# A decoder layer in which most PE transposes are replaced by 32x32 block transposes on VectorE and a pass through DRAM

## The chip, the cores and the metric

The kernel runs on one core of a Trainium2 chip. The metric is the device time of one execution in microseconds (us); the time before is 2097.85 us, the median of 3 runs (2097.81 to 2097.95). The engines are named as the profile names them: PE (TensorE) with PEld for its weight loads, DVE (VectorE), ACT (ScalarE), POOL (GpSimd) and SP (SyncE), which issues the DMAs.

## The reference

One decoder layer on 256 tokens, D_MODEL 2048, all in float32:

```
x = x + 1/2 * SwiGLU_1(rms(x))              # D_FF 5632: (silu(x@wg) * (x@wu)) @ wd
h = rms(x); proj = h @ w_in                 # q | k | v | u | v_sg | gate_att | gate_sg
  q, k: rotary on the first quarter of each of 12 heads (128 wide)
  branch A: causal dilated window attention, 3 groups of 4 heads, merged by denominators
  branch B: u * (W_s LN(v_sg) + b), W_s lower triangular
  merged = sigmoid(gate_att) * (A @ w_att_out) + sigmoid(gate_sg) * (B @ w_sg_out)
x = x + merged @ w_out
x = x + 1/2 * SwiGLU_2(rms(x))
out = rms(x) * final_norm
```

## The kernel before

**Products in three passes.** Each float32 matrix product is made of three float32r products: the left side is split into `hi` and `lo`, the weights into `wh` and `wl`, and PE adds hi·wh, hi·wl and lo·wh (lines 145 to 147). Activations are the stationary side, so they have to lie transposed in SBUF: 128 features on the partitions, the 256 tokens along the row. Weights are the moving side, 512 columns at a time.

**The list of half units.** All products of the layer are cut into 776 half units, numbered `i`: two 128-row slices of a weight, times two token halves, times three passes, which is 12 matmuls of 128x512. A gate, up or w_in product has 8 half units for its 512 columns, a down product 12 or 10. The main loop (lines 719 to 729) issues for each `i` the 12 matmuls, then the callbacks that were put at `i` with `at`, then the split of the weights of half unit `i + 4` (line 130 on ACT writes `wh`, line 131 on DVE writes `wl`). There are four `wh`/`wl` buffers, so the split of `i + 4` waits until PE is done with half unit `i`. A 1 MB weight load (`raw`, three buffers, line 121 on SP) is issued as soon as the split that frees its buffer stands in the list. Every engine takes its instructions in the order of this list.

**The transposes.** When a result is ready, PE transposes it in 128x128 pieces against an identity matrix into PSUM, and ACT and DVE bring it back as `hi` and `lo`. With `e` the last half unit of the product that gave the result:
- feed-forward (22 chunks of 512 columns, `post_up`): DVE multiplies at `e+1`, PE transposes 8 pieces at `e+2` (line 263), `split_psum` at `e+3` (lines 152 and 153);
- the two inner norms (`residual`, four chunks of 512 each, for n = 1 and 2): 8 transposes at `e+2` (line 179), the copies with the norm's gain at `e+3` (lines 184 and 186);
- q and k (`post_qk`, three chunks each): rotary at `e+2`, 8 transposes at `e+3` (line 434), plain copies at `e+4`;
- the merge (`post_merge`, four chunks): 8 transposes at `e+2` (line 583), `split_psum` at `e+3`.

The transposed feed-forward chunks `hhi` and `hlo` are the left side of the down products, which follow at once: half unit `e+1` of a down product reads slices 0 and 1, `e+2` slices 2 and 3, and so on. The feed-forward is done in two parts, of 6 chunks (24 slices) and of 5 chunks (20 slices). The first norm of the layer, attention and the gating branch have transposes of their own.

Of the kernel before, what the change touches and what calls it, by code (L numbers as in the profile page):

```python
# [8 lines left out]
F32 = mybir.dt.float32  # L9
F32R = mybir.dt.float32r  # L10
BF16 = mybir.dt.bfloat16
AF = mybir.ActivationFunctionType
# [29 lines left out]
def layer(ctx: ExitStack, tc: tile.TileContext, a, out):  # L42
# [2 lines left out]
    big = ctx.enter_context(tc.tile_pool(name="big", bufs=1))  # L45
    sb = ctx.enter_context(tc.tile_pool(name="sb", bufs=1))
    ps = ctx.enter_context(tc.tile_pool(name="ps", bufs=1, space=PSUM))
    ctx.enter_context(tc.manual_schedule())

    def mm_bank(name):  # L50
# [2 lines left out]
    def tp_bank(name):  # L53
        return ps.tile([P, NC], F32, tag="tp", bufs=4, name=name)
# [96 lines left out]
    def split_psum(hi, lo, src):  # L151
        ACT.activation(hi, src, AF.Copy)
        DVE.tensor_tensor(lo, src, hi.bitcast(F32), op=OP.subtract)


    xT = {}

    def norm_open(n):
# [30 lines left out]
    def residual(e, n, c, banks, scale, norm):  # L189
        cs = slice(c * NC, (c + 1) * NC)  # L190

        def add():
            for t in range(NT):
                DVE.scalar_tensor_tensor(two(x[:, t, cs]), banks[t], scale, two(x[:, t, cs]),  # L194
                                         op0=OP.mult, op1=OP.add)
            if norm:
                if c == 0:
                    norm_open(n)
                norm_squares(n, c)

        at(e + 1, add)
        if not norm:
            return
        got = {}

        def tr():
            for kk in range(2):
                ks = [4 * c + 2 * kk, 4 * c + 2 * kk + 1]
                got[kk] = ks, norm_transposes(f"{n}_{ks[0]}", ks)
            if c == 3:  # L210
                norm_rstd(n)

        def ev():
            for kk in range(2):
                norm_evac(n, *got[kk])

        at(e + 2, tr)
        at(e + 3, ev)


    def ffn(wg, wu, wd, down_post):
        halves = ((0, 6), (6, 11))
        for hf, (f0, f1) in enumerate(halves):
            st = {}

            def lhs_x():
                return xT["hi"], xT["lo"]

            def lhs_h(st=st):
                return st["hi"], st["lo"]  # L230

            for f in range(f0, f1):
                def post_gate(e, banks, st=st):
                    st["sg"] = sg = sb.tile([P, NT, NC], F32, tag="tmp", bufs=2, name=f"sg{e}")

                    def go():
                        rstd = xT["rstd"]
                        for t in range(NT):
                            ACT.activation(two(sg[:, t]), banks[t], AF.Silu, scale=rstd[:, t:t + 1])

                    at(max(e + 1, 11), go)

                def post_up(e, banks, st=st, f=f, f0=f0):
                    sg = st["sg"]
                    kl = 4 * (f - f0)
                    if f == f0:
                        st["hi"] = big.tile([P, 24, S], F32R, tag="A", name=f"hhi{e}")
                        st["lo"] = big.tile([P, 24, S], F32R, tag="B", name=f"hlo{e}")
                    got = {}

                    def mul():
                        rstd = xT["rstd"]
                        for t in range(NT):
                            DVE.scalar_tensor_tensor(two(sg[:, t]), banks[t], rstd[:, t:t + 1], two(sg[:, t]),  # L254
                                                     op0=OP.mult, op1=OP.mult)

                    def tr():
                        for kk in range(2):
                            b = tp_bank(f"ht{e}_{kk}").rearrange("p (j s) -> p j s", j=2)
                            for j in range(2):  # L260
                                for t in range(NT):
                                    k = 2 * kk + j
                                    PE.transpose(b[:, j, t * P:(t + 1) * P], sg[:, t, k * P:(k + 1) * P], ident)  # L263
                            got[kk] = b

                    def ev():
                        for kk in range(2):
                            ks = slice(kl + 2 * kk, kl + 2 * kk + 2)
                            split_psum(st["hi"][:, ks], st["lo"][:, ks], got[kk])

                    at(e + 1, mul)
                    at(e + 2, tr)
                    at(e + 3, ev)

                gemm(wg, f * NC, 0, KD, lhs_x, post_gate)
                gemm(wu, f * NC, 0, KD, lhs_x, post_up)
            for c in range(4):
                gemm(wd, c * NC, f0 * NC, 4 * (f1 - f0), lhs_h,
                     lambda e, banks, c=c, hf=hf: down_post(e, c, banks, hf == 1))
# [124 lines left out]
    def post_qk(key, gi):  # L404
        def post(e, banks):
            q = sb.tile([P, NT, NSLOT, HD], F32, tag="tmp", bufs=2, name=f"{key}{gi}")
            if ("qk", 0) not in mix:
                mix["qk", 0] = big.tile([P, 2, NG, S], F32, tag="A", name="qkT")
            dst = mix["qk", 0][:, 0 if key == "q" else 1, 4 * gi:4 * gi + 4]
            got = {}  # L410

            def cp():
                for t in range(NT):
                    ACT.activation(q[:, t].rearrange("p (a h) d -> p a (h d)", a=2), banks[t], AF.Copy,
                                   scale=xT["rstd"][:, t:t + 1])

            def rope():
                for t in range(NT):
                    tmp = sb.tile([P, NSLOT, 32], F32, tag="rope", bufs=2, name=f"rp{e}_{t}")
                    x1, x2 = q[:, t, :, 0:16], q[:, t, :, 16:32]  # L420
                    c2 = cs_t[:, t, 0:1, :].to_broadcast([P, NSLOT, 32])
                    s1 = cs_t[:, t, 1:2, 0:16].to_broadcast([P, NSLOT, 16])
                    s2 = cs_t[:, t, 1:2, 16:32].to_broadcast([P, NSLOT, 16])
                    DVE.tensor_tensor(tmp[:, :, 0:16], x2, s1, op=OP.mult)
                    DVE.tensor_tensor(tmp[:, :, 16:32], x1, s2, op=OP.mult)
                    DVE.tensor_tensor(q[:, t, :, 0:32], q[:, t, :, 0:32], c2, op=OP.mult)
                    DVE.tensor_tensor(q[:, t, :, 0:32], q[:, t, :, 0:32], tmp, op=OP.add)

            def tr():
                for hh in range(2):  # L430
                    b = tp_bank(f"{key}t{gi}_{hh}").rearrange("p (j s) -> p j s", j=2)
                    for j in range(2):
                        for t in range(NT):
                            PE.transpose(b[:, j, t * P:(t + 1) * P], q[:, t, 2 * hh + j], ident)  # L434
                    got[hh] = b

            def ev():
                ACT.activation(dst[:, 0:2], got[0], AF.Copy)
                DVE.tensor_copy(dst[:, 2:4], got[1])

            at(e + 1, cp)
            at(e + 2, rope)
            at(e + 3, tr)
            at(e + 4, ev)
            if key == "k" and gi == 2:
                attention(e + 21)
        return post
# [117 lines left out]
    def post_merge(c):  # L565
        def post(e, banks):
            post_mul("ga")(e, banks)
            ga, gs = mix["ga"], mix["gs"]
            got = {}
            if c == 0:  # L570
                mix["mhi"] = big.tile([P, KD, S], F32R, tag="A", name="mhi")
                mix["mlo"] = big.tile([P, KD, S], F32R, tag="C", name="mlo")

            def add():
                DVE.tensor_tensor(ga, ga, gs, op=OP.add)

            def tr():
                for kk in range(2):
                    b = tp_bank(f"mt{c}_{kk}").rearrange("p (j s) -> p j s", j=2)
                    for j in range(2):  # L580
                        k = 2 * kk + j
                        for t in range(NT):
                            PE.transpose(b[:, j, t * P:(t + 1) * P], ga[:, t, k * P:(k + 1) * P], ident)  # L583
                    got[kk] = b

            def ev():
                for kk in range(2):
                    ks = slice(4 * c + 2 * kk, 4 * c + 2 * kk + 2)
                    split_psum(mix["mhi"][:, ks], mix["mlo"][:, ks], got[kk])

            at(e + 1, add)
            at(e + 2, tr)
            at(e + 3, ev)
        return post
# [188 lines left out]
```

## Time and profile before

| what | value |
|---|---|
| median of 3 runs | 2097.85 us |
| profiled execution | 2098.01 us |
| its span, first to last instruction | 2096.3 us |
| granted TensorE clock, mean | 0.999 |
| PE busy | 2083.5 us (99%) |
| DVE busy | 1127.0 us (54%) |
| ACT busy | 965.2 us (46%) |
| DMA | 416.40 MB, mean 199 GB/s |

The span holds the work of all engines; the 1.7 us between it and the execution's time lie around it. The matmuls of PE are pipelined, so the durations of single matmuls overlap, and what one costs is read from the distance between starts. The granted clock is that of full speed (2.4 GHz) in nearly all of the span. Busy times of DVE and ACT can be added up.

### The profile page before, as it was taken

To read this page: it belongs to the slowest core of one execution; us is meant where nothing else is said; L and a number is where in the kernel's file an instruction comes from. 1 tells how busy PE (TensorE), PEld (TensorE's weight loads), DVE (VectorE), ACT (ScalarE), POOL (GpSimd) and SP (SyncE) were. 2 spreads that over 40 slices of the span, in tenths; PEclk is the share of its full clock that TensorE was granted. 3 is DMA by queue.
4 is the path that set the end of the run, shared out by engine and by line. 5 is a ranking of instruction groups with operands and counts; after the bars stand their busy time and mean duration, and the time that the engine had idled before them with its cause. 6 is when DMAs were issued, how large, how long until landed. Compare 5 with 4: busy or idle time off the path is not lost.

```text
span 2096.3 us, 24121 instructions
## 1 busy us (share of the span) xinstructions
PE 2083.5 (99%) x9897; PEld 1825.1 (87%) x9897; DVE 1127.0 (54%) x1141; ACT 965.2 (46%) x1090; POOL 9.4 (0%) x13
## 2 busy tenths in 40 slices
PE   9999999999999999999999999999999999999998
PEld 7888888888888888888888888888888888888887
DVE  5555555455555555655555555555555555555554
ACT  6444444444445544444454444544444444444443
POOL 0000000000000000000000000000000000000000
PEclk9999999999999999999999999999999999999999
DMA  7666655666675666556545566556665566666654
GB/s 262 200 201 201 201 200 202 201 201 201 195 251 188 201 201 201 173 189 200 190 146 186 201 201 201 201 192 198 200 199 196 200 202 204 200 200 220 201 200 141
DMA packets 210759, 416.40 MB, mean 199 GB/s; under 512 B 6685, under 2 KB 10457, under 8 KB 210521
## 3 DMA queue, kind: packets, MB, share of 16 engines
q1 hardware_dynamic: 210648, 414.87, 59.8%
q8 instruction: 77, 1.26, 0.2%
q14 instruction: 34, 0.27, 0.0%
HBM read 412.74 MB, written 2.10 MB: 198 GB/s over the span
## 4 chain that ended last, share of the span: by engine, by line
PE 99%; DMA 0%; issue 0%; ACT 0%; DVE 0%; SPq 0%; ACTq 0%; POOLq 0%; POOL 0%
PE mm L146 32%; PE mm L145 32%; PE mm L147 32%; PE ht L263 1%; PE xt L179 0%; DMA raw<-in_ffn_w_gate_dram 0%; PE sc L473 0%; PE sp L376 0%; PE mt L583 0%; PE pv L521 0%; PE pv L520 0%; PE pv L516 0%; PE sc L471 0%; PE kt L434 0%; PE pt L500 0%
## 5 line engine op out<-in xcount | busy, mean ns | idle before, releaser
L131 DVE TENSOR_TENSOR wl<-raw,wh 128x1024 fp32r<-128x1024 f32 (+1 forms) x777 | 949.8, 1223 | 937.7 <-ACT wh L130 935.8
L130 ACT ACTIVATE wh<-raw 128x1024 fp32r<-128x1024 f32 (+1 forms) x777 | 818.7, 1055 | 1070.9 <-PE mm L147 1055.7
L145 PE MATMUL mm<-wh,xhi 128*128 128x512 f32 x2144 | 818.2, 382 | 0.6 <-ACT wh L130 0.6
L146 PE MATMUL mm<-wl,xhi 128*128 128x512 f32 x2144 | 813.0, 379 | 0.5 <-DVE wl L131 0.5
L147 PE MATMUL mm<-wh,xlo 128*128 128x512 f32 x2144 | 812.6, 379 | 0.0
L146 PEld LDWEIGHTS mm<-wl,xhi 128*128 128x128 f32 x2144 | 405.3, 189 | 57.8 <-DVE wl L131 1.4
L147 PEld LDWEIGHTS mm<-wh,xlo 128*128 128x128 f32 x2144 | 405.2, 189 | 57.4
L145 PEld LDWEIGHTS mm<-wh,xhi 128*128 128x128 f32 x2144 | 405.3, 189 | 57.2 <-ACT wh L130 1.0
L145 PE MATMUL mm<-wh,hhi 128*128 128x512 f32 x704 | 267.6, 380 | 0.0
L146 PE MATMUL mm<-wl,hhi 128*128 128x512 f32 x704 | 266.8, 379 | 0.0
L147 PE MATMUL mm<-wh,hlo 128*128 128x512 f32 x704 | 266.8, 379 | 0.0
L147 PEld LDWEIGHTS mm<-wh,hlo 128*128 128x128 f32 x704 | 133.1, 189 | 18.9
L145 PEld LDWEIGHTS mm<-wh,hhi 128*128 128x128 f32 x704 | 133.1, 189 | 18.7
L146 PEld LDWEIGHTS mm<-wl,hhi 128*128 128x128 f32 x704 | 133.1, 189 | 18.6
L145 PE MATMUL mm<-wh,mhi 128*128 128x512 f32 x128 | 48.8, 382 | 0.0
L146 PE MATMUL mm<-wl,mhi 128*128 128x512 f32 x128 | 48.5, 379 | 0.0
L147 PE MATMUL mm<-wh,mlo 128*128 128x512 f32 x128 | 48.5, 379 | 0.0
L145 PE MATMUL mm<-wh,uT 128*128 128x512 f32 x96 | 36.7, 383 | 0.0
L146 PE MATMUL mm<-wl,uT 128*128 128x512 f32 x96 | 36.4, 379 | 0.0
L147 PE MATMUL mm<-wh,uT 128*128 128x512 f32 x96 | 36.4, 379 | 0.0
L254 DVE SCALAR_TENSOR_TENSOR sg<-mm,rstd,sg 128x512 f32<-128x512 f32 x44 | 30.9, 743 | 0.0
L165 ACT ACTIVATE junk<-x 128x512 bf16<-128x512 f32 x30 | 18.9, 629 | 21.3 <-DVE x L194 15.1
(140 smaller groups left out, 668.0 us busy)
## 6 DMA issues: line engine op xcount, KB each, us to landing
raw<-in_w_in_dram SPq DMA_DIRECT2D x92, 1024.0 KB, 4.9
raw<-in_ffn_w_up_dram SPq DMA_DIRECT2D x88, 1024.0 KB, 5.0
raw<-in_ffn_w_down_dram SPq DMA_DIRECT2D x88, 1024.0 KB, 5.0
raw<-in_ffn_w_gate_dram SPq DMA_DIRECT2D x85, 1024.0 KB, 5.1
raw<-in_w_out_dram SPq DMA_DIRECT2D x16, 1024.0 KB, 5.0
raw<-in_w_sg_out_dram SPq DMA_DIRECT2D x12, 1024.0 KB, 5.0
raw<-in_w_att_out_dram SPq DMA_DIRECT2D x4, 1024.0 KB, 5.0
raw<-in_ffn_w_gate_dram SPq DMA_DIRECT2D x5, 512.0 KB, 7.9
```

The source lines that it names most:

```text
L130: ACT.activation(wh[:, k], r[:, k], AF.Copy)
L131: DVE.tensor_tensor(wl[:, k], r[:, k], wh[:, k].bitcast(F32), op=OP.subtract)
L145: PE.matmul(o, hi[:, k, tt], in_turn(wh[:, jj]), start=first, stop=False)
L146: PE.matmul(o, hi[:, k, tt], in_turn(wl[:, jj]), start=False, stop=False)
L147: PE.matmul(o, lo[:, k, tt], in_turn(wh[:, jj]), start=False, stop=last)
L165: ACT.activation(junk, x[:, t, c * NC:(c + 1) * NC], AF.Square, accum_out=ss[n][:, t, c:c + 1])
L254: DVE.scalar_tensor_tensor(two(sg[:, t]), banks[t], rstd[:, t:t + 1], two(sg[:, t]), op0=OP.mult, op1=OP.mult)
L263: PE.transpose(b[:, j, t * P:(t + 1) * P], sg[:, t, k * P:(k + 1) * P], ident)
```

## The change

A helper `turn` takes the place of the transposes in `post_up`, in `post_qk`, and in chunks 0 to 2 of the inner norms and of the merge: 22 + 6 + 6 + 3 = 37 places. Chunk 3 of the norms and of the merge stays on PE, as do the first norm, attention and the gating branch. A turn does this:
- at its first point, two DVE instructions transpose the 32x32 blocks of a 128x1024 result (one per token half) into a tile `d` in SBUF, and SP writes `d` to a DRAM tile in one DMA of 512 KB;
- three half units later, SP reads it back in four DMAs of 128 KB, each to 32 partitions, in runs of 1 KB;
- six half units after the first point, ACT and DVE write `hi` and `lo` (or, for q and k, plain copies) from the SBUF tile that was read back. For the norms four ACT instructions multiply by the gain before that.

```
+    def turn(i, name, src, dst, ev):
+        got = {}
+        def blocks():
+            d = sb.tile([P, 4, 4, NT, 32], F32, tag="gate", bufs=2, name=f"bt{name}")
+            v = src()
+            for t in range(NT):
+                DVE.transpose(d.rearrange("p j k t b -> p t k j b")[:, t],
+                              v[:, t].rearrange("p (k j b) -> p k j b", j=4, b=32))
+            m = got["m"] = dram.tile([P, 4, S], F32, tag="turn", name=f"bm{name}")
+            SP.dma_start(m, d.rearrange("p j k t b -> p j (k t b)"))
+        def back():
+            got["e"] = e = dst()
+            m = got["m"].rearrange("(i a) j r -> j a i r", a=32)
+            for j in range(4):
+                SP.dma_start(e[32 * j:32 * j + 32].rearrange("p t c -> p (t c)").rearrange("p (i r) -> p i r", i=4),
+                             m[j])
+        at(i, blocks)
+        at(i + 3, back)
+        at(i + 6, lambda: ev(got["e"].rearrange("p t c -> p (t c)").rearrange("p (i q b) -> p q i b", i=4, b=32)))
+    def turned(ap):
+        return ap.rearrange("p k (t i b) -> p (k t) i b", t=NT, b=32)
...
@@ residual @@
+        if c < 3:
+            def evac(src):
+                for j in range(4):
+                    v = src[:, 2 * j:2 * j + 2]
+                    k = 16 * n + 4 * c + j
+                    ACT.activation(v, v, AF.Copy, scale=gcols[:, k:k + 1])
+                ks = slice(4 * c, 4 * c + 4)
+                split_psum(turned(xT["hi"][:, ks]), turned(xT["lo"][:, ks]), src)
+            turn(e + 2, f"x{n}_{c}", lambda: x[:, :, cs],
+                 lambda: sb.tile([P, NT, NC], F32, tag="gate", bufs=2, name=f"xt{n}_{c}"), evac)
+            return
...
@@ post_up @@
-                    at(e + 2, tr)
-                    at(e + 3, ev)
+                    turn(e + 2, f"h{e}", lambda: sg, lambda: sg, ev)
...
@@ post_qk @@
-                ACT.activation(dst[:, 0:2], got[0], AF.Copy)
-                DVE.tensor_copy(dst[:, 2:4], got[1])
+            def ev(src):
+                ACT.activation(turned(dst[:, 0:2]), src[:, 0:4], AF.Copy)
+                DVE.tensor_copy(turned(dst[:, 2:4]), src[:, 4:8])
...
-            at(e + 3, tr)
-            at(e + 4, ev)
+            turn(e + 3, f"{key}{gi}", lambda: flat(q), lambda: flat(q), ev)
...
@@ post_merge @@
+            if c < 3:
+                turn(e + 2, f"m{c}", lambda: ga, lambda: ga,
+                     lambda src: split_psum(turned(mix["mhi"][:, 4 * c:4 * c + 4]),
+                                            turned(mix["mlo"][:, 4 * c:4 * c + 4]), src))
+                return
```

The three places below all belong to the last chunk of the first feed-forward, whose up product ends with half unit 223. Names carry the half unit: `wh226` is the weight split of 226, `mm224_0` the PSUM bank of the down product that begins at 224.

On PE, between half units 225 and 226, before:

```order
L145 MATMUL mm224_1_4295<-wh225_4256,hhi159_3108 128x512
L146 MATMUL mm224_1_4295<-wl225_4257,hhi159_3108 128x512
L147 MATMUL mm224_1_4295<-wh225_4256,hlo159_3109 128x512
L263 MATMUL ht223_0_4337<-ident_74,sg215_4149 128x128 [waits DVE_49] x2
L263 MATMUL ht223_0_4337<-ident_74,sg215_4149 128x128 x2
L263 MATMUL ht223_1_4342<-ident_74,sg215_4149 128x128 x4
L145 MATMUL mm224_0_4294<-wh226_4274,hhi159_3108 128x512 [waits Activation_49]
L146 MATMUL mm224_0_4294<-wl226_4275,hhi159_3108 128x512
```

The same place now:

```order
L146 MATMUL mm224_1_4267<-wh225_4228,hhi159_3092 128x512
L147 MATMUL mm224_1_4267<-wl225_4229,hhi159_3092 128x512
L148 MATMUL mm224_1_4267<-wh225_4228,hlo159_3093 128x512
L146 MATMUL mm224_0_4266<-wh226_4246,hhi159_3092 128x512 [waits Activation_49]
L147 MATMUL mm224_0_4266<-wl226_4247,hhi159_3092 128x512 [waits DVE_49]
L148 MATMUL mm224_0_4266<-wh226_4246,hlo159_3093 128x512
```

The eight transposes are gone, and nothing has come in their place on PE.

On SP, around the weight loads `raw116` to `raw119`, before (`sgw`, `lng` and `lnb` are constants of the mixer that are loaded once, here):

```order
L302 DMA sgw_4310<-in_sg_w_dram 128x12x128
L309 DMA lng_4313<-in_sg_ln_g_dram 128x1536
L309 DMA lnb_4314<-in_sg_ln_b_dram 128x1536
L121 DMA raw116_4319<-in_ffn1_w_down_dram 128x4x512 [waits DMAHW1_49,DVE_49]
L121 DMA raw117_4367<-in_ffn1_w_down_dram 128x4x512 [waits DMAHW2_49,DVE_49]
L121 DMA raw118_4401<-in_ffn1_w_down_dram 128x4x512 [waits DMAHW3_49,DVE_49]
```

The same place now (`bth223` is the tile of block transposes, `bmh223` the DRAM tile):

```order
L338 DMA lnb_4286<-in_sg_ln_b_dram 128x1536
L122 DMA raw116_4291<-in_ffn1_w_down_dram 128x4x512 [waits DMAHW3_49,DVE_49]
L168 DMA bmh223_4312<-bth223_4309 128x1024 [waits DMAHW4_49,DVE_49]
L122 DMA raw117_4330<-in_ffn1_w_down_dram 128x4x512 [waits DMAHW5_49,DVE_49]
L174 DMA sg215_4119<-bmh223_4312 32x4x256 [waits DMAHW6_49,DMAHW4_49]
L174 DMA sg215_4119<-bmh223_4312 32x4x256 [waits DMAHW7_49]
L174 DMA sg215_4119<-bmh223_4312 32x4x256 [waits DMAHW0_49]
L174 DMA sg215_4119<-bmh223_4312 32x4x256 [waits DMAHW1_49]
L122 DMA raw118_4368<-in_ffn1_w_down_dram 128x4x512 [waits DMAHW2_49,DVE_49]
L122 DMA raw119_4402<-in_ffn1_w_down_dram 128x4x512 [waits DMAHW3_49,DVE_49]
```

One write and four reads have come between the weight loads; the first read waits for the write to land, and `raw118` stands behind it.

On ACT, the copy that writes `hhi` for this chunk, before:

```order
L130 ACTIVATE wh228_4321<-raw114_4238 128x1024 [waits DMAHW2_49,DVE_49,PE_49]
L130 ACTIVATE wh229_4347<-raw114_4238 128x1024 [waits DVE_49,PE_49]
L152 ACTIVATE hhi159_3108<-ht223_0_4337 128x512 [waits PE_49]
L152 ACTIVATE hhi159_3108<-ht223_1_4342 128x512 [waits PE_49]
L130 ACTIVATE wh230_4369<-raw115_4272 128x1024 [waits DMAHW3_49,DVE_49,PE_49]
L130 ACTIVATE wh231_4385<-raw115_4272 128x1024 [waits DVE_49,PE_49]
```

And now:

```order
L131 ACTIVATE wh233_4386<-raw116_4291 128x1024 [waits DVE_49,PE_49]
L131 ACTIVATE wh234_4404<-raw117_4330 128x1024 [waits DMAHW5_49,DVE_49,PE_49]
L153 ACTIVATE hhi159_3092<-sg215_4119 128x1024 [waits DMAHW6_49,DMAHW7_49,DMAHW1_49,DMAHW0_49]
L131 ACTIVATE wh235_4422<-raw117_4330 128x1024 [waits DVE_49,PE_49]
L131 ACTIVATE wh236_4440<-raw118_4368 128x1024 [waits DMAHW2_49,DVE_49,PE_49]
```

The copy has moved from behind the split of 229 to behind that of 234, and it waits for the four reads. Its partner on DVE (`hlo159`) has moved likewise, to between `wl234` and `wl235`. On PE the first half unit that reads these slices is 232, and its third matmul has a wait that it did not have before:

```order
L146 MATMUL mm224_0_4266<-wh232_4370,hhi159_3092 128x512 [waits Activation_49]
L147 MATMUL mm224_0_4266<-wl232_4371,hhi159_3092 128x512 [waits DVE_49]
L148 MATMUL mm224_0_4266<-wh232_4370,hlo159_3093 128x512 [waits DVE_49]
L146 MATMUL mm224_1_4267<-wh232_4370,hhi159_3092 128x512
L147 MATMUL mm224_1_4267<-wl232_4371,hhi159_3092 128x512
L148 MATMUL mm224_1_4267<-wh232_4370,hlo159_3093 128x512
```

## Rows read from the trace of the kernel before

**Rows 1.** The page: PE's busy time, and the chain by engine.

```profile
PE 2083.5 (99%) x9897; PEld 1825.1 (87%) x9897; DVE 1127.0 (54%) x1141; ACT 965.2 (46%) x1090; POOL 9.4 (0%) x13
...
PE 99%; DMA 0%; issue 0%; ACT 0%; DVE 0%; SPq 0%; ACTq 0%; POOLq 0%; POOL 0%
```

**Rows 2.** Waits of PE: total us, times, longest us.

```profile
PE mm L145 <- ACT wh L130: 0.6, 1, 0.6
PE mm L146 <- DVE wl L131: 0.5, 2, 0.2
```

**Rows 3.** Groups on PE: line, out<-in, count | busy us, mean ns | idle before.

```profile
L263 PE MATMUL ht<-ident,sg 128*128 128x128 f32 x176 | 22.8, 273 | 0.0
...
L179 PE MATMUL xt<-ident,x 128*128 128x128 f32 x64 | 8.3, 273 | 0.0
...
L583 PE MATMUL mt<-ident,ga 128*128 128x128 f32 x32 | 4.1, 272 | 0.0
...
L434 PE MATMUL kt<-ident,k 128*128 128x128 f32 x24 | 3.1, 273 | 0.0
```

**Rows 4.** Timeline, PE around half units 225 and 226: start us, length us, instruction.

```profile
606.22 0.38 PE L147 MATMUL mm<-wh,hlo 128*128 128x512 f32 x1
...
606.44 1.04 PE L263 MATMUL ht<-ident,sg 128*128 128x128 f32 x8
...
607.53 0.38 PE L146 MATMUL mm<-wl,hhi 128*128 128x512 f32 x1
607.53 0.19 PEld L147 LDWEIGHTS mm<-wh,hlo 128*128 128x128 f32 x1
...
607.74 0.38 PE L147 MATMUL mm<-wh,hlo 128*128 128x512 f32 x1
```

**Rows 5.** Timeline, ACT at the same place (wh228 is at 604.05).

```profile
604.05 1.06 ACT L130 ACTIVATE wh<-raw 128x1024 fp32r<-128x1024 f32 x1 [1.53 <-PE mm L147]
606.64 1.06 ACT L130 ACTIVATE wh<-raw 128x1024 fp32r<-128x1024 f32 x1 [1.53 <-PE mm L147]
607.60 1.07 ACT L152 ACTIVATE hhi<-ht 128x512 fp32r<-128x512 f32 x2
610.10 1.06 ACT L130 ACTIVATE wh<-raw 128x1024 fp32r<-128x1024 f32 x1 [1.43 <-PE mm L147]
```

**Rows 6.** Timeline, DVE at the same place (wl228 is at 605.13).

```profile
605.13 1.23 DVE L131 TENSOR_TENSOR wl<-raw,wh 128x1024 fp32r<-128x1024 f32 x1
607.73 1.22 DVE L131 TENSOR_TENSOR wl<-raw,wh 128x1024 fp32r<-128x1024 f32 x1 [1.37 <-ACT wh L130]
608.87 1.28 DVE L153 TENSOR_TENSOR hlo<-ht,hhi 128x512 fp32r<-128x512 f32 x2
```

**Rows 7.** Groups on DVE that work inside SBUF, by form.

```profile
L632 DVE TENSOR_TENSOR x<-x,fing 128x512 f32<-128x512 f32 x6 | 4.2, 692 | 0.8 <-ACT junk L165 0.6
...
L653 DVE TENSOR_SCALAR x<-x,rf 128x512 f32<-128x512 f32 x2 | 1.0, 486 | 1.3 <-POOL rf L647 1.3
...
L170 DVE TENSOR_SCALAR ms<-ms 128x2 f32<-128x2 f32 x3 | 0.5, 170 | 0.1
```

**Rows 8.** A group on ACT: the norms' copies.

```profile
L184 ACT ACTIVATE xhi<-xt,gcols 128x256 fp32r<-128x256 f32 x32 | 12.4, 466 | 0.0
```

**Rows 9.** DMA issues: out<-in, engine, count, KB each, median us to landing.

```profile
raw<-in_ffn_w_down_dram SPq DMA_DIRECT2D x88, 1024.0 KB, 5.0
...
out_dram<-x SPq DMA_DIRECT2D x8, 256.0 KB, 3.2
...
lnb<-in_sg_ln_b_dram SPq DMA_DIRECT2D x1, 768.0 KB, 8.4
```

**Rows 10.** The eight loads of x (256 KB each, runs of 1 KB), by tile.

```profile
DMA to landing us min/median/max: 3.3/7.3/7.9
```

**Rows 11.** Timeline, SP: the constants and raw116 at half unit 224.

```profile
603.05 0.43 SPq L309 DMA_DIRECT2D lnb<-in_sg_ln_b_dram  x1
603.80 5.56 SPq L121 DMA_DIRECT2D raw<-in_ffn_w_down_dram  x2
```

More of the change, by code (lines that the diff above doesn't have):

```diff
@@ L47, in layer @@
     ps = ctx.enter_context(tc.tile_pool(name="ps", bufs=1, space=PSUM))
+    dram = ctx.enter_context(tc.tile_pool(name="dram", bufs=2, space=bass.MemoryType.DRAM))
     ctx.enter_context(tc.manual_schedule())
@@ L248, in post_up @@
                         st["lo"] = big.tile([P, 24, S], F32R, tag="B", name=f"hlo{e}")
-                    got = {}
                     def mul():
@@ L255, in mul @@
                                                      op0=OP.mult, op1=OP.mult)
[L257 to L269, printed above, removed]
+                    def ev(src):
+                        hi, lo = st["hi"][:, kl:kl + 4], st["lo"][:, kl:kl + 4]
+                        split_psum(turned(hi), turned(lo), src)
                     at(e + 1, mul)
-                    at(e + 2, tr)
-                    at(e + 3, ev)
+                    turn(e + 2, f"h{e}", lambda: sg, lambda: sg, ev)
                 gemm(wg, f * NC, 0, KD, lhs_x, post_gate)
@@ L409, in post, with flat @@
             dst = mix["qk", 0][:, 0 if key == "q" else 1, 4 * gi:4 * gi + 4]
-            got = {}
+            def flat(v):
+                return v.rearrange("p t h d -> p t (h d)")
             def cp():
@@ L427, in rope, with ev @@
                     DVE.tensor_tensor(q[:, t, :, 0:32], q[:, t, :, 0:32], tmp, op=OP.add)
[L429 to L437, printed above, removed]
-                ACT.activation(dst[:, 0:2], got[0], AF.Copy)
-                DVE.tensor_copy(dst[:, 2:4], got[1])
+            def ev(src):
+                ACT.activation(turned(dst[:, 0:2]), src[:, 0:4], AF.Copy)
+                DVE.tensor_copy(turned(dst[:, 2:4]), src[:, 4:8])
             at(e + 1, cp)
             at(e + 2, rope)
-            at(e + 3, tr)
-            at(e + 4, ev)
+            turn(e + 3, f"{key}{gi}", lambda: flat(q), lambda: flat(q), ev)
             if key == "k" and gi == 2:
@@ L575, in add @@
                 DVE.tensor_tensor(ga, ga, gs, op=OP.add)
+            at(e + 1, add)
+            if c < 3:
[3 more added lines that the diff above has]
+                return
             def tr():
@@ L589, in ev @@
                     split_psum(mix["mhi"][:, ks], mix["mlo"][:, ks], got[kk])
-            at(e + 1, add)
             at(e + 2, tr)
```

## The prediction

> **What bounds the kernel now.** I read the page first: PE is busy 2083.5 of 2096.3 us, and the chain that ended last lies on PE for 99% of its length [rows 1]. Then the waits: in the whole span PE waits for a weight split 0.6 us once and 0.5 us in two pieces [rows 2]. So PE runs without a pause, and an instruction taken out of its queue shortens the run by what it holds PE for, unless a new wait appears. ACT (46%) and DVE (54%) follow PE: the split of half unit i+4 starts when PE has finished i. Last I read the timelines of the three engines at one place, the end of the last up product of the first feed-forward [rows 4 to 6], since the change must be judged by what each engine is doing within a few half units.
>
> **What is removed.** The groups on PE show 176 transposes of feed-forward chunks, 64 of the inner norms, 32 of the merge, 24 of k (q has as many) [rows 3]. All 176, 48 of the 64, 24 of the 32, and 24 + 24 go: 296, in 37 groups of eight. What does a group hold PE for? Matmuls start 0.215 us apart (607.53 to 607.74). From the L147 at 606.22 to the L146 at 607.53 there are 1.31 us with the eight transposes between; without them it is two steps (L147 to L145 to L146), 0.43 us. So eight cost 0.88 us [rows 4]. ACT confirms it: its splits start when PE ends a half unit, 2.59 us apart (604.05 to 606.64), and 3.46 us apart over the transposes (606.64 to 610.10), 0.87 us more [rows 5]. I take 0.87: 37 x 0.87 = 32.2 us off PE; by 0.88 it is 32.6.
>
> The duration of a transpose, 273 ns [rows 3], must not be used for this: eight of them span 1.04 us in all [rows 4], since they overlap: 0.11 us (0.87 by eight) is the price of one. The Trainium skill, in "TensorE: Matmul & The Clock Gate", section "Part 4: PE-mode transpose", gives about 275 ns for a 128x128 transpose (bfloat16) inside a kernel. The trace agrees with this as a duration. Taken as a price, 296 of them would be some 81 us, an estimate by that page (rival 4).
>
> **What is added to DVE and ACT.** 74 block transposes of 128x512 on DVE. The trace has none. The nearest rows in SBUF at this size are 0.486 us for one source and 0.692 us for two [rows 7]; I take 0.69, as DVE writes here in pieces of 32. The far end: if each of the 16 blocks cost as much as a tiny DVE instruction, 0.17 us [rows 7], one would be 2.7 us. At 0.69 a turn adds 1.38 us to DVE, 51 us over the run, to an engine that is busy 54% of it. Cover: wl starts 1.09 us after wh (606.64 to 607.73) and lasts 1.22, so wl of half unit i+4 is ready 2.3 us after PE ends i, while PE asks for it three half units on, 7.77 us after. That leaves 5.4 us, just what a pair at the far end takes (2 x 2.7): no cost at either end. Behind the transposes on DVE stands only the next wl, whose reader is PE, with that cover.
>
> The copies move from `e+3` to `e+8`. One 128x1024 copy takes the place of two of 128x512, on ACT about 1.06 us as wh does [rows 5], on DVE 1.22 us as wl does [rows 6]: no more than before. The norms add one ACT copy per chunk: four scalings of 0.47 us [rows 8] and 1.06 us, 2.9 us in one half unit, still within 5.4 us, at six places.
>
> **What is added to SP and the DMAs.** Per turn one write and four reads, 1 MB in all. Weight load raw116 is issued at 603.80 [rows 11]; its reader wh232 comes four half units after wh228 (604.05 + 4 x 2.59 = 614.4), 10.6 us later, and a load lands in 5.0 [rows 9]. The turn's 1 MB can hold it up by about one more load's 5.0, so the splits never wait for weights; even if they did, PE has its 5.4 us. The first read waits on SP for the write to land, with raw118 queued behind it. In the steady state that load is due two half units after raw117, and the write, issued about 1.2 us before raw117, has some 6 us; 256 KB written to DRAM land in 3.2 [rows 9], so 512 KB behind part of a load in 3.2 to 5.0. No loss there.
>
> **Where the read-back meets ACT and DVE.** At the place in rows 5 and 6, wl228 ends at 606.36 and the block transposes at 607.74; call it t0. wh234 starts at 604.05 + 6 x 2.59 = 619.59, and the copy to `hhi` 0.96 us later (as 606.64 to 607.60): 12.8 us after t0. The read-back is there after the write (3.2 to 5.0), four issues of about 0.43 [rows 11], and a landing of 3.3 to 7.9, the bounds of the x loads, which also run in pieces of 1 KB [rows 10]: 8.2 to 14.6 us. So the copy finds its data 4.6 us early or waits up to 1.8 us. A wait on ACT or DVE delays the next splits, which have 5.4 us: nothing is lost at 35 of the 37 turns.
>
> Two turns have no such room. In each feed-forward the last chunk of the second part ends at `e`, and its slices 16 and 17 are read by PE at `e+9`, while the copy stands at `e+8`. PE starts `e+9` 2.39 us after wh234 starts (a half unit less the 0.20 us between them). `hi` is ready 0.96 + 1.06 = 2.0 us after it, in time. `lo` follows wl234 on DVE: it starts 1.14 us after it (607.73 to 608.87), 2.23 after wh234, and ends at 3.46. The third matmul loads its `lo` weights 0.21 us ahead [rows 4], at 2.6, and must wait to 3.5: 0.9 us lost, twice, 1.8 us. If the read-back is late, the lateness comes on top: up to 2.7 us each. At the first of the two places the mixer's constants are in the queue as well: `lnb`, issued at 603.05, lands 8.4 us later at 611.45 [rows 9, 11], 3.7 after t0, and the write is behind it; that end may be 2 us later still. So the two cost 1.8 us, with bounds 0 and 7.4. In the first part of each feed-forward slices 20 and 21 are read at `e+11`, two half units later, and lose nothing.
>
> **Sum.** Profiled execution 2098.01 - 32.2 + 1.8 = 2067.6; the median of the runs is 0.16 lower, so 2067.5 us. Bounds of this case: 2065.3 (32.6 off, no wait) to 2073 (all bounds at their slow end).
>
> **Rivals.**
> 1. *The read-back comes late everywhere, and the kernel gets slower.* ACT's in-order queue is the place: behind the waiting copy stands the next wh, and PE stops when the copy is more than 5.4 us late, at t0 + 18.2. A turn has eaten its 0.87 us at t0 + 19.1; from there on the kernel is slower. That is reached if the four reads, 32 partitions each, land one after another in more than 3.4 to 3.7 us each (18.2 or 19.1, less 4.4 for the write, by four). For it: the x loads took 3.3 to 7.9 [rows 10]. Against: those were issued together and their median counts queueing; four reads go out in 1.7 us. At 4.5 us each, turns end at t0 + 22.4, 4.2 late: 37 x 4.2 = 155, 2221 us; at 3.6 each about half the gain is returned, 2083. The Trainium skill speaks for it: "VectorE: DVE Perf Modes", section "The three transpose paths", warns that a plain DMA that transposes by strides is 19 times slower than the crossbar's when the innermost destination stride is large. Here DVE turns the blocks and the DMA moves runs of 1 KB; no run so far shows such a DMA.
> 2. *The block transposes are slow.* Past 2.7 us each the cover is gone; past 3.15 (5.4 + 0.87, halved) the kernel is slower. At 4 us: 37 x (8 - 5.4) = 96, 2162 us. Against it the rows at this size, 0.49 and 0.69 us [rows 7].
> 3. *No change:* PE is not what bounds, and the splits set its pace. Then 2098. Against it the waits of PE, 1.1 us in all [rows 2].
> 4. *More than forecast:* a transpose costs its 273 ns, and 296 of them bring 80.8 us: 2017. Only the durations speak for it, the starts against.
>
> **Chances and range.** Forecast 0.78, rival 1 0.10 (half of it slower, half between 2073 and 2094), rival 2 0.04, rival 3 0.05, rival 4 0.03. A measurement can tell 0.2% (4.2 us) from no change. Faster: 0.78 + 0.05 + 0.03 = 0.86; within 0.2%: 0.05; slower: 0.05 + 0.04 = 0.09. The range 2063.5 to 2078 takes in the forecast's bounds and the start of rival 1's partial return; the rest of the rivals, under 0.2, is left out.
>
> **What would show it.** Right: no L263 and L434 groups on PE, ACT's splits 2.59 us apart over the old places, PE's waits about 1 us longer at two down products and nowhere else, DVE up by some 40 to 50 us, DMA traffic by 39 MB. A block transpose near 0.7 us, a write landing in 3 to 5, reads before t0 + 12.8. Wrong: waits of PE for wh or wl spread over the 37 turns, ACT waiting for the read DMAs by more than 5 us, or weight loads that land later than the splits ask for them.

## The result and the profile after

The changed kernel takes 2067.11 us (median of 4 runs, 2066.53 to 2068.01), the kernel before 2097.83 (4 runs). The ratio is 0.9854, with a 95% interval of 0.9837 to 0.9871: faster by 30.7 us. Forecast were 2067.5 us and a range of 2063.5 to 2078. The profiled execution took 2066.57, its span 2064.8 us.

The page of the kernel after: busy time of the engines, what HBM moved, and the chain by engine, which answer to [rows 1]:

```profile
PE 2051.4 (99%) x9601; PEld 1794.1 (87%) x9601; DVE 1164.2 (56%) x1172; ACT 970.8 (47%) x1071; POOL 9.4 (0%) x13
...
HBM read 432.14 MB, written 21.50 MB: 220 GB/s over the span
...
PE 98%; DMA 1%; DVE 0%; issue 0%; ACT 0%; SPq 0%; ACTq 0%; POOLq 0%; POOL 0%; DVEq 0%
```

PE has 296 instructions less (9897 to 9601) and 32.1 us less busy time, and still bounds the run. DVE has 37 us more, a little under the 40 to 50 that were named as a sign.

The timeline of ACT at the end of the first chunk of the first feed-forward, after (start, length, instruction):

```profile
55.97 1.06 ACT L131 ACTIVATE wh<-raw 128x1024 fp32r<-128x1024 f32 x1 [1.53 <-PE mm L148]
58.56 1.06 ACT L131 ACTIVATE wh<-raw 128x1024 fp32r<-128x1024 f32 x1 [1.53 <-PE mm L148]
61.15 1.06 ACT L131 ACTIVATE wh<-raw 128x1024 fp32r<-128x1024 f32 x1 [1.53 <-PE mm L148]
...
71.51 1.06 ACT L131 ACTIVATE wh<-raw 128x1024 fp32r<-128x1024 f32 x1 [1.53 <-PE mm L148]
72.47 1.04 ACT L153 ACTIVATE hhi<-sg 128x1024 fp32r<-128x1024 f32 x1
```

The splits are 2.59 us apart, also at the third, where 3.46 us lay before [rows 5]; the copy to `hhi` follows its split with no wait.

SP at the same place: the write at 59.52, a weight load, the four reads at 62.25, the next weight load.

```profile
59.52 0.35 SPq L168 DMA_DIRECT2D bmh<-bth  x1
60.90 0.37 SPq L122 DMA_DIRECT2D raw<-in_ffn_w_up_dram  x1
62.25 1.77 SPq L174 DMA_DIRECT2D sg<-bmh  x4
66.08 0.39 SPq L122 DMA_DIRECT2D raw<-in_ffn_w_up_dram  x1
```

The groups that are new, from the views of DVE's groups and of the DMA issues (KB each, median us to landing), and the landings of the writes alone:

```profile
L165 DVE STREAM_TRANSPOSE bth<-sg 128x512 f32<-128x512 f32 x44 | 28.5, 687 | 0.0
...
bmh<-bth SPq DMA_DIRECT2D x22, 512.0 KB, 3.3
sg<-bmh SPq DMA_DIRECT2D x88, 128.0 KB, 4.9
...
DMA to landing us min/median/max: 2.7/3.3/8.1
```

A block transpose takes 0.687 us (0.69 was taken, from a neighbour), a write lands in 3.3 us, a read in 4.9. The last read of the four is issued by 64.0 and lands about 4.9 us later, near 68.9 (an estimate from the median), 9.4 us after the block transposes ended; ACT comes to the copy at 72.47, 13 us after. The forecast had 8.2 to 14.6 and 12.8.

What PE's weight loads wait for, after 30 us (the waits before that belong to the start of the kernel), which answers to [rows 2]:

```profile
PEld mm L148 <- DVE hlo L154: 1.9, 2, 1.0
PEld gc L732 <- issue: 0.3, 1, 0.3
PEld mm L146 <- ACT hhi L153: 0.2, 1, 0.2
```

Two waits for `hlo`, 1.0 and 0.9 us, with 0.2 us for `hhi` at the first of the two places, and at no other place a wait for what was turned. At the first of the two, at the end of the first feed-forward, ACT finds the read-back just landed, and the reads were issued 8.1 us after the write, as the constants of the mixer and a weight load were ahead of it (ACT, then SP; the run consts_early below tests this):

```profile
610.23 1.06 ACT L131 ACTIVATE wh<-raw 128x1024 fp32r<-128x1024 f32 x1 [1.53 <-PE mm L148]
611.44 1.07 ACT L153 ACTIVATE hhi<-sg 128x1024 fp32r<-128x1024 f32 x1 [0.16 <-DMA sg<-bmh]
```

```profile
598.24 0.33 SPq L168 DMA_DIRECT2D bmh<-bth  x1
599.62 0.38 SPq L122 DMA_DIRECT2D raw<-in_ffn_w_down_dram  x1
606.36 1.75 SPq L174 DMA_DIRECT2D sg<-bmh  x4
```

### The profile page after: what moved, and what is told of

Read it like the earlier page. It is cut to its first block, busy times and chain, and to the rows that moved or that the text cites. A ratio compares the mean times of both kernels' runs of the same rounds, so it can differ in the third digit from the quotient of the medians.

```text
span 2064.8 us, 23874 instructions
## 1 busy us (share of the span) xinstructions
PE 2051.4 (99%) x9601; PEld 1794.1 (87%) x9601; DVE 1164.2 (56%) x1172; ACT 970.8 (47%) x1071; POOL 9.4 (0%) x13
## 4 chain that ended last, share of the span: by engine, by line
PE 98%; DMA 1%; DVE 0%; issue 0%; ACT 0%; SPq 0%; ACTq 0%; POOLq 0%; POOL 0%; DVEq 0%
PE mm L148 32%; PE mm L147 32%; PE mm L146 32%; DMA bmh<-bth 0%; DMA raw<-in_ffn_w_gate_dram 0%; PE sc L495 0%; PE sp L405 0%; DMA sg<-bmh 0%; ACT wh L131 0%; PE pv L543 0%; PE pv L542 0%; PE pv L538 0%; PE sc L493 0%; PE spt L421 0%; PE pt L522 0%
```

## The experiments

Theory A is that of the prediction: PE's queue sets the time, eight transposes hold PE for 0.87 us, and what was added is covered but for two waits at the last chunks. Its rivals are that the price per transpose is another, that the additions cost PE something that the gain hides, and that the covers are other than worked out. Ratios are to the kernel before on the same chip.

**The changed kernel again (after_again), and with two edits.** No edit in the first.

> The changed kernel once more, on the same chip as the next three, for their comparison. Theory A (PE's queue sets the time, 0.87 us per group of eight transposes, and all that was added is covered but for two waits of 0.9 to 1.0 us in front of the third matmul of a half unit): 2066.5 to 2068, with runs that differ by up to 1.5 us as they did before. If the spread is from the chip and not from the kernel, the kernel before would spread as much here; it spread 0.4.

Measured: 2067.59 us (2067.09 to 2068.37), ratio 0.9855 (0.9838 to 0.9871). The changed kernel's four runs spread by 1.3 us, the seven of the kernel before beside them by 1.0 (2097.55 to 2098.54), so the spread is not the changed kernel's alone. Its profiled run took 2068.37, and PE's weight loads waited there for

```profile
PEld mm L148 <- DVE hlo L154: 1.9, 2, 1.0
...
PEld mm L146 <- ACT hhi L153: 1.1, 1, 1.1
```

So in this run the read-back behind the constants came about 1 us later than in the first one, and PE waited for `hhi` as well. This is half of the 1.8 us between the two profiled runs; the other half lies before the first turn: the split that stood at 55.97 in the first run stands at 56.86.

The last chunk of each feed-forward copied one half unit earlier, and the constants loaded 8 half units earlier (last_early; `...` marks what is left out of a line):

```
-    def turn(i, name, src, dst, ev):
+    def turn(i, name, src, dst, ev, lag=6):
...
-        at(i + 6, lambda: ev(got["e"]...
+        at(i + lag, lambda: ev(got["e"]...
...
-                    turn(e + 2, f"h{e}", lambda: sg, lambda: sg, ev)
+                    turn(e + 2, f"h{e}", lambda: sg, lambda: sg, ev, 5 if f == 10 else 6)
...
-    at(11 * 16 + 24 + 24, mixer_consts)
+    at(11 * 16 + 24 + 16, mixer_consts)
```

> The last chunk of each feed-forward is copied one half unit earlier (lag 5 in place of 6), and the mixer's constants are loaded 8 half units earlier. Theory A: both waits of PE for hlo go (1.0 + 0.9 us in the profile), 2065 to 2065.5, and since the late read-back behind the constants is gone, a spread under 0.6 us. Rival B (the wait only moves: the copy meets the read-back before it has landed, and PE waits for that): no gain, 2066.5 or more, with ACT waiting for the reads at these two turns.

Measured: 2065.41 us (2065.10 to 2065.50), ratio 0.9845 (0.9830 to 0.9859). PE waits for nothing of the turns any more. This version beats both kernels, by 2.2 us against the changed one on the same chip, with a spread of 0.4.

The constants moved alone (consts_early, the last line of the diff above):

> Only the mixer's constants are loaded 8 half units earlier; the last chunk keeps lag 6. Theory C on the spread (at the end of the first feed-forward the write queues behind the constants, 8.1 us to landing, and the read-back comes just at the copy, in some runs later): the write lands in about 3.3 us, PE's two waits stay at 0.9 to 1.0, the time is the lowest of the changed kernel's, 2066.5, in all runs, spread under 0.6. If the spread has another source, it stays at about 1.5 us.

Measured: 2067.03 us (2066.82 to 2067.15), ratio 0.9853 (0.9838 to 0.9867). The longest write landed in 4.1 us in place of 8.1, PE's two waits stayed (0.9 and 0.9), the spread fell to 0.33. The time is not the lowest of the changed kernel's: the start took longer in the profiled run (the split at 55.97 in the first run stands at 56.62), with 2.8 us of waits for weight splits in the first 50 us. So the late write comes from the constants, and the two waits do not. What the constants do to the spread is not settled by four runs: no_turn below has no read-back at all, and its four spread by 1.7 us.

**No turn at all (no_turn).**

```
     def turn(i, name, src, dst, ev):
-        ...                        # blocks() and back(), with the DMAs, and their three at(...)
+        def go():
+            e = dst()
+            ev(e.rearrange("p t c -> p (t c)").rearrange("p (i q b) -> p q i b", i=4, b=32))
+        at(i + 1, go)
...
@@ residual @@
-                    ACT.activation(v, v, AF.Copy, scale=gcols[:, k:k + 1])
+                    xs = x[:, :, k % 16 * P:(k % 16 + 1) * P].rearrange("p t (i b) -> p t i b", b=32)
+                    ACT.activation(v, xs, AF.Copy, scale=gcols[:, k:k + 1])
```

> Leaves out the block transposes, the write and the reads: the copies at e+3 (q and k e+4) take the untransposed tile, so the numbers are not the reference's. It shows what the removal of 296 transposes alone brings. Theory A: 2097.85 less 37 x 0.87 = 2065.6 (2065.3 to 2065.8), 1.5 us under the changed kernel, that is its two waits. If the turn's transfers and DVE work cost PE more than those two waits, this run is lower than that; if a transpose costs its 273 ns, it is at 2017.

Measured: 2065.54 us (2065.32 to 2067.04), ratio 0.9847 (0.9832 to 0.9862). From the split of half unit 20 to the last matmul the profiles give

| kernel | split of 20 | last matmul starts | between |
|---|---|---|---|
| before | 56.57 | 2086.85 | 2030.28 |
| after | 55.97 | 2055.51 | 1999.54 |
| last_early | 56.55 | 2054.43 | 1997.88 |
| no_turn | 56.84 | 2054.72 | 1997.88 |

With no transposes and no turns PE is 32.40 us shorter, 0.876 us per group of eight. With the turns and the last chunk early it is the same to 0.01 us: in these profiles, 74 block transposes and 37 passes through DRAM cost PE nothing (the medians, 2065.41 and 2065.54, agree). In the changed kernel the two waits cost 1.66 of it. The rival price of 273 ns per transpose (2017 us) is out.

**The transposes kept on PE beside the turns (pe_kept).**

```
+        def dummy():
+            ...         # eight PE transposes of src() into banks that nobody reads
+        at(i, dummy)
         at(i, blocks)
```

> The changed kernel, with the 37 groups of eight PE transposes left where they were, into PSUM banks that nobody reads. All that was added is there, nothing is taken off PE. Theory A (PE's queue): the changed kernel's 2067.1 to 2067.6 and 32.2, 2099.3 to 2099.8, so 1.5 to 2 us above the kernel before: that is the price of the addition, two waits of about 1 us. If the added transfers and DVE work cost PE something all along that the saving hides, it is above 2102.

Measured: 2101.08 us (2099.47 to 2104.71), ratio 1.0014 (1.0004 to 1.0024), which is 0.8 to 5.0 us above the kernel before. The whole gain goes back to PE's queue. The median lies 1.3 us above theory A's 2099.8 and below the 2102 of its rival. Besides the two waits for `hlo`, the kept transposes of q and k waited 1.3 us in the profiled run (0.6 for a weight split, 0.7 for rotary results). The runs were spread over 5 us, and the highest is above 2102, so this run alone does not decide; last_early against no_turn does.

**Norms and merge on PE again (norm_merge_pe).** `if c < 3` becomes `if c < 0` in `residual` and `post_merge`.

> Norms and merge go back to PE; only the feed-forward chunks and q and k are turned, 28 of 37 places. Theory A: each place is worth 0.87 us: 9 x 0.87 = 7.8 us above the changed kernel, 2074.9 to 2075.5. If the norms' turns (one more ACT copy each) or the merge's cost as much as they bring, it is at 2067.

Measured: 2075.2 us (2074.86 to 2075.73), ratio 0.9892 (0.9877 to 0.9907): 7.6 us above after_again; nine places at 0.87 give 7.8.

**Block transposes four and six times (dve4, dve6).**

```
-            for t in range(NT):
+            for t in [t for t in range(NT) for _ in range(4)]:     # or 6
                 DVE.transpose(...)
```

> Each block transpose is issued four times into the same tile: 8 of 0.69 us per turn, 5.5 us on DVE in place of 1.4. Theory A: wl of the next half unit is ready some 4 us later, still 1.4 us before PE wants it, and the read-back 4 us later, at the copy or up to 1 us behind it, inside 5.4 us: 2067 to 2071, the only loss at the two last chunks (the read-back is late there, up to 1 to 2 us each). Rival D (DVE has no such cover): 37 x 4.1 = 152 us more, 2219.

> Each block transpose six times: 12 of 0.69 us per turn, 8.2 us on DVE. Theory A: wl of the next half unit starts when DVE is free, 6.8 us later than now, is ready 1.4 us after PE wants it, so PE loses about 1.5 us at each turn: 37 x 1.5 = 55, and a little at the last chunks: 2123 (2105 to 2140). Rival D (no cover): 37 x 6.9 = 255 more, 2322. If DVE's delay is hidden further, under 2080.

Measured: dve4 2110.56 us (2107.53 to 2110.72), ratio 1.0057 (1.0042 to 1.0072); dve6 2206.21 (2203.12 to 2209.34), ratio 1.0516 (1.0500 to 1.0532). Both are slower than theory A said, and far below rival D. Two stretches of dve4 (start and end, length, busy time and count of PE, PEld, DVE, ACT and POOL, then granted clock, DMA share and GB/s; the first stretch lies in the first feed-forward, the second holds q and k):

```profile
50.00:600.00 550.00, 550.00 (x2550) 481.63 (x2549) 344.43 (x337) 244.92 (x243) 0.00 (x0) 1.00 0.69 224
860.00:1010.00 150.00, 133.56 (x583) 113.20 (x582) 101.08 (x151) 57.66 (x65) 0.00 (x0) 0.95 0.63 208
```

In the feed-forward PE is never idle: there eight block transposes, 5.77 us in one piece, are covered, as worked out. In dve6 the twelve take 8.76 us, and in the same stretch each of the ten turns costs 2.0 us where 1.5 was expected. At q and k of dve4 PE stood still for 16 us. SP's and ACT's waits in that stretch:

```profile
SPq L168 <- DVE btk L165: 45.2, 3, 15.8
SPq L168 <- DVE btq L165: 39.6, 3, 14.3
```

```profile
ACT wh L131 <- DMA raw<-in_w_in_dram: 42.5, 6, 8.5
```

The write of q and k is put at `e+3` and not at `e+2`, and so it stands on SP directly ahead of a weight load that is due then. SP waits for the block transposes, the load stands behind it, and ACT waits for such loads 7.1 us on average. But the chain that ended last does not run over these loads; it runs over the turns themselves (start, length, what; pieces between are left out):

```profile
869.59 2.99 DMA bmq<-btq
...
874.03 8.90 DMA q<-bmq
...
883.58 1.25 ACT k L445 x2
...
885.80 1.23 DVE wl L132
...
892.16 1.31 DVE btk L165 x2
...
895.73 2.99 DMA bmk<-btk
```

ACT's copy waits for the read-back, the work on k stands behind that copy on ACT and DVE, and the next block transposes stand behind this work. PE waits for the `wl` that follows them (20.1 us in nine waits of its weight loads). The writes of q and k lie 21.1 us apart on average in the changed kernel and 25.4 in dve4: one turn does not fit between two any more. Theory A had looked at the cover of a single turn, and not at a delay that runs into the next one. How much the held weight loads add was not separated by a run. In the changed kernel, with 1.4 us of block transposes, none of this costs anything.

The rest of the miss is at the norms (8.3 us of PE's idle time between 1330 and 1440 us) and in the clock. The granted clock was 0.95 in the stretch of q and k, against 1.00 in the feed-forward: after PE had stood still for 3.1 of 6 us (890 to 896), it was 0.50, the lower level (1.2 GHz), from 896 to 902. Over the whole run the mean was 0.994 against 0.999 in the changed kernel, an estimated 10 us, and PE was busy for 14 us longer with the same 9601 instructions; it was idle for 27 us more. In dve6 the mean clock was 0.983, PE busy 41 us longer and idle 98 us more, 2.7 per turn. Theory A had nothing for the clock.

**The copies earlier (lag3, lag1).**

```
-        at(i + 3, back)
-        at(i + 6, lambda: ev(...
+        at(i + 2, back)           # lag1: i + 1
+        at(i + 3, lambda: ev(...  # lag1: i + 1
```

> Every turn is copied three half units earlier: the reads stand at i+2 in place of i+3, the copies at i+3 in place of i+6. The copy on ACT then stands about 5.0 us after the block transposes, the data is there at about 9.3 as now, so ACT waits some 3 to 4.5 us at each of the 37 turns. Theory A (PE has 5.4 us of splits ahead): PE loses nothing of this, and the two waits for hlo at the last chunks go, since the copies come before half unit e+9: 2065 to 2066. Rival E (a wait of ACT for the reads costs PE what it lasts): 37 x 3.5 = 130 more, 2197.

> Reads and copies both at i+1: the reads stand on SP right behind the write and ahead of the next weight load, the copy on ACT at about the moment at which the block transposes end. ACT is held for about 8 us at each turn. Theory A: that is 2 to 3 us over the cover of 5.4, 37 x 2.5 = 92, 2158 (2140 to 2185). Rival E (no cover): 37 x 8 = 300, 2365. If the cover is much deeper than worked out, under 2080.

Measured: lag3 2095.93 us (2090.09 to 2104.18), ratio 0.9996 (0.9982 to 1.0011); lag1 2213.42 (2205.73 to 2216.08), ratio 1.0544 (1.0526 to 1.0562). Neither hits theory A's number, lag3 by 30 us. At the first chunk of lag3 the timeline of ACT shows the wait that was expected,

```profile
64.28 1.06 ACT L131 ACTIVATE wh<-raw 128x1024 fp32r<-128x1024 f32 x1 [1.53 <-PE mm L148]
69.83 1.06 ACT L153 ACTIVATE hhi<-sg 128x1024 fp32r<-128x1024 f32 x1 [4.50 <-DMA sg<-bmh]
```

and PE's weight loads waited 1.9 us in the ten first chunks of that feed-forward together and not at all at q and k, so waits of 4 to 5 us are covered, and rival E (2197) falls. The rest was lost at the norms and behind the constants. PE's weight loads in the stretch 590 to 720 us, and ACT's waits there:

```profile
PEld mm L146 <- ACT wh L131: 9.4, 4, 3.8
PEld mm L147 <- DVE wl L132: 4.9, 4, 1.3
```

```profile
ACT xt L238 <- DMA xt<-bmx: 22.2, 3, 8.8
ACT hhi L153 <- DMA sg<-bmh: 9.3, 1, 9.3
```

At the norms ACT waits 7.4 us on average, and four scalings follow before the copy: more than the 5.4 us that PE has ahead. At the first of these norm chunks the read-back is as early as at the feed-forward (9.7 us after the write was issued, against 9.8), but ACT stands at it earlier, 3.5 us after that issue and not 5.3; at the other two it comes after 12.1 and 12.4 us, for which no cause was tried. lag1 is past the cover nearly everywhere and lost 3.9 us per turn (146 us by 37, against the changed kernel) where 2.5 was expected. Of the 148 us between the profiled runs PE was idle for 90, 2.4 per turn, as theory A said; for the other 58 the same 9601 instructions kept it busy longer, at a mean granted clock of 0.978 against 0.999, which theory A had left out.

**The gating branch turned too (gating_turned).** On top of last_early, three more turns replace 24 transposes of the gating branch.

```
-            at(e + pg + 2, tr)
-            at(e + pg + 3, ev)
+            if pg % 2:
+                turn_u(e + pg + 2, pg)      # as turn, on mix["u"], eight reads of 64 KB
```

> The kernel with the last chunk copied early (2065.4), and the gating branch's 24 transposes turned as well: three more turns, two half units apart, each with one write and eight reads of 64 KB. Theory A: 3 x 0.87 = 2.6 us less, 2062.8. Rival F (SP: the writes wait for DVE and the reads for the writes, three turns and the first of q follow on each other, and the weight loads between them are late by more than the 5.6 us they can be): the gain is lost or more, 2065 to 2080, with ACT waiting for weights there.

Measured: 2070.17 us (2069.28 to 2071.30), ratio 0.9868 (0.9854 to 0.9882): 4.8 us slower than last_early, in the range of rival F, and with its sign. ACT's waits in the stretch 840 to 960 us:

```profile
ACT wh L131 <- DMA raw<-in_w_in_dram: 17.1, 4, 5.5
ACT uT L153 <- DMA uv<-bmu: 10.8, 3, 4.7
ACT qkT L478 <- DMA k<-bmk: 9.4, 2, 5.2
ACT qkT L478 <- DMA q<-bmq: 8.8, 2, 4.7
```

The weight loads stand behind the writes and reads of four turns that follow on each other, and ACT waits for them up to 5.5 us. The chain that ended last runs there over two of these loads (9.6 and 7.3 us) and then over the read-backs of q and k (up to 9.7), so both held PE up; no run separates them.

## Why the prediction was right

- **The removal.** 37 groups at 0.87 us, 32.2 us, were forecast; 32.40 were measured, 0.876 each. The distance between starts was the right price; the duration of 273 ns, which makes 80.8 us of 296, was not.
- **The two last chunks.** 0.9 us each was forecast, from the row of a copy on DVE behind its split; the profile has 1.0 and 0.9, and their removal gave 1.66 us between two fixed points of the timeline. The first of them was also named as the one where the constants might make the read-back late, by up to 2 us; the sum took nothing for it. It was 0.2 us late in one profile and 1.1 us in another, so the forecast within half a microsecond is partly luck.
- **The block transposes.** 0.687 us each, taken as 0.69. Their cover holds in the feed-forward (none lost at 5.77 us, 2.0 at 8.76).
- **The transfers.** The write landed in 3.3 (3.2 to 5.0 was taken), the read-back 9.4 us after the block transposes (8.2 to 14.6). The read-backs of k were the latest: ACT waited for them up to 1.9 us (up to 1.8 was allowed for), inside its cover. The Trainium skill, in "VectorE: DVE Perf Modes", section "The three transpose paths", warns of plain DMAs that transpose by strides. No run here has such a DMA; the reads in runs of 1 KB that were used took no more than 9 us in the changed kernel.
- **What was right only for this size.** "No cost at either end" of the block transposes, up to 2.7 us each, holds in the feed-forward but not at q and k, where the turns follow on each other more closely: 5.8 us per turn cost PE 16 us in that stretch, and more by the lower clock. The forecast did not depend on it, since 1.4 us do not reach that far. The cover of 5.4 us also does not hold for the copy at the norms, where ACT has more to do.
- **Rivals 1 to 4.** No wait of PE spread over the turns (1, 2), the gain is there (3), and it is not the 80 us of the durations (4). One figure of rival 1 does not come out of its own terms: at 3.6 us per read a turn would end 0.6 us past t0 + 18.2, which returns two thirds of the gain and not half, and gives some 2088 us in place of 2083.

## What to carry to other kernels

Where one engine runs without a pause, price what leaves its queue by the distance between starts over that piece, on that engine and on one that follows it, and then look for the few places at which the replacement's result is wanted before the lookahead has passed: here two of 37. The detour of about 9 us through DRAM was free here where all in-order queues on its way had that much lookahead; check the queue of the engine that issues the transfers as well, for what stands behind a transfer that waits, and where several detours follow on each other, whether one ends before the next begins. Once the bounding engine has to stand still, add what the lower clock costs to the waits: by the two mean clocks an estimated 46 of 148 us in lag1. When a late stage has no room, moving its copy by one step can be worth more than the next piece of work taken off the bounding engine.

## What the runs showed of the hardware

- Eight 128x128 float32 transposes in a row, at the higher clock level (2.4 GHz, granted 1.00), hold PE for 0.876 us among matmuls of 128x512, though each lasts 273 ns.
- DVE transposes a 128x512 float32 tile in 32x32 blocks in 0.687 us, as long as a two-source instruction of that size (0.692 us [rows 7]), with a destination in pieces of 32 elements.
- A 512 KB write to DRAM landed in 2.7 us at best and in 8.1 behind 2.6 MB of constants and a 1 MB weight load, issued in the 8.6 us before it (4.1 at most with the constants elsewhere). A read of 128 KB into 32 partitions landed in 4.9 us (median, feed-forward), and in 8.5 for k, where at the first place two 1 MB loads had been issued in the 3.6 us before the reads. The landings of the twelve reads of k, and ACT's waits for them:

```profile
k<-bmk SPq DMA_DIRECT2D x12, 128.0 KB, 8.5
...
ACT qkT L461 <- DMA k<-bmk: 5.2, 3, 1.9
```

- The clock fell where PE had stood still: in dve4 it was 0.50 (1.2 GHz) from 896 to 902 us, after PE had been idle for 3.1 us of the 6 before, and at that level matmuls of 128x512 started 0.43 us apart in place of 0.215.
- The start of the kernel differs from run to run by about 1 us (55.97 to 56.86 us for the same split), half of the difference between the two profiled runs of the changed kernel.
